# Value projections at 512 columns, last products by column halves, and a queue offset for every stick-breaking head

## The chip, the cores and the metric

One core of one Trainium2 chip runs the kernel. The metric is the device time of one execution in microseconds (us); below, TensorE is PE, VectorE is DVE, ScalarE is ACT, GpSimd is POOL, and SP is the engine that issues most transfers.

## The reference, cut to what matters

Two layers (DEPTH 2) work on 512 tokens of width 1024. Each layer is a half-step SwiGLU, a gated mix of three attentions, and another half-step SwiGLU, each between two RMS norms. All is float32.

```python
for l in range(DEPTH):
    f = _swiglu(_rmsnorm(h, ffn1_pre_g[l]), ffn1_w_gate[l], ffn1_w_up[l], ffn1_w_down[l])
    h = h + 0.5 * _rmsnorm(f, ffn1_post_g[l])
    u = _rmsnorm(h, mix_pre_g[l])
    proj = u @ w_in[l]
    q_sb, k_sb, v_sb, q_fx, k_fx, v_fx, f_logit, q_mem = jnp.split(proj, split_at, axis=-1)
    o_sb = stick_breaking(q_sb, k_sb, v_sb)          # 8 heads of 64
    o_fx = forgetting(q_fx, k_fx, v_fx, log_f)       # 8 heads of 64
    k_mem, v_mem = jnp.split(mem_n @ w_mem_kv[l], 2, axis=-1)
    o_mem = memory(q_mem, k_mem, v_mem)              # 4 heads of 128, 256 memory rows
    merged = g_sb * (o_sb @ w_br_sb[l]) + g_fx * (o_fx @ w_br_fox[l]) + g_mem * (o_mem @ w_br_mem[l])
    h = h + _rmsnorm(merged @ w_out[l], mix_post_g[l])
    f = _swiglu(_rmsnorm(h, ffn2_pre_g[l]), ffn2_w_gate[l], ffn2_w_up[l], ffn2_w_down[l])
    h = h + 0.5 * _rmsnorm(f, ffn2_post_g[l])
```

The values v_sb are 512 columns of `w_in` wide (all eight heads), v_fx as well, and v_mem is the second 512 columns of `w_mem_kv`.

## The kernel before

Every large matrix product is made with three matmuls: each operand is split into a high part (a rounded copy, made by ACT) and a low part (the residue, made by DVE), and `mm3` adds high x high, high x low and low x high in PSUM. `split` makes the two parts. A weight slice of 512 KB is a `Unit`: SP loads it into one of two raw buffers (`raw`), ACT casts it to `wh`, DVE makes the residue `wl` (four buffers each). A square of 128 x 128 numbers is the stationary operand of a matmul; the moving one is up to 512 columns wide.

The order of PE's work is written out by a queue, `Queue` (`Q`). A job in it is a set of units and a generator that emits matmuls; `Q.step` emits the next piece, loads the units of the job that begins, and loads up to four units ahead. Attention heads are chains: a generator yields ("pe", us) for PE work that it just emitted and ("wait", us) for the queued PE work that is to be put in before its next part. `Q.weave` puts chain and queue together, up to a limit in the queue; `Q.past` runs the queue past a job and some microseconds on; `Q.until` runs it to a mark. The engines then run in order, so these offsets set how much other PE work lies between the parts of a head.

The mixing stage of a layer `l`, in order:

- `mem_kv` adds the memory keys (two jobs `keys`, tiles `pmk`, 256 columns of memory rows moving) and the memory values (two jobs `values`, tiles `pmv`, each 256 value columns wide, by `vproj`). The second values job is added from `mixing` by `rest`.
- `mixing` adds the memory queries (`pqm`), then for every head pair p a q and a k projection (`project`, tiles `pq`, `pk`), value projections (`project_v`), and gated merges (`merge`, gate tiles `pg`, product tiles `pb`). Values of two head pairs are made at a time, 256 columns, by `v_half` and `vproj` (tiles `pv`); two token tiles share a bank of PSUM. The forgetting branch's first value job also makes the forget logits and is 264 columns wide (`v_gates`).
- `run` in `mixing` weaves the heads: four memory heads (`mem_head`), eight stick-breaking heads (`stick_head`, pair p and head j, tiles `zs`, `ts`, `pts`, `pvs`), eight forgetting heads (`fox_head`). In a stick-breaking head PE makes the scores `zs` (L966); ACT and DVE turn them into weights in `ts` (L971 to L983); PE transposes them into `pts` (L952, in `transposed`); ACT and DVE split these; PE multiplies with the values into `pvs` (L939, in `attend`).

Between `zs` and `pts` the weave puts in W_SB0 of queued work, plus an entry of W_MORE for three of the heads, and between `pts` and `pvs` W_SB1:

```python
    W_SB0, W_SB1 = 12.0, 4.7
    W_MORE = {(0, 0): -5.5, (NP - 1, 0): 2.0, (NP - 1, 1): 1.0}
```

`down` makes a SwiGLU's last products (tiles `pdc` in the second SwiGLU) and the output projection. Its last two token tiles are made one after the other by `late`, then `Sub.result` squares and scales a tile's half (L549, L554), `rstd` makes the norm's factor, and `Sub.residual` adds into `hm` (L572) and stores (L573).

At the start, `begin` loads tiles of x on SP (L1366, L1369), `Sub.gains` loads the first gain row in two pieces (`grow`, L536) and PE spreads it over the partitions (`gqx`, L540); `warm(n)` issues n matmuls whose result is not used (L1359); `turn` transposes a normed tile (`utx`, L1389).

Of the kernel before, what the change touches and what calls it, by code (L numbers as in the profile page):

```python
# [17 lines left out]
P = 128  # L18
# [4 lines left out]
def kernel(  # L23
# [469 lines left out]
    def rstd(st, a, b=None):  # L493

        s, m, y, w = st[:, a:a + 1], st[:, 3:4], st[:, 4:5], st[:, 5:6]
        if b is None:
            nc.scalar.activation(y, s, AF.Ln, bias=eps_t[:])
            nc.vector.tensor_scalar(m, s, D * EPS, None, ALU.add)
        else:
            nc.vector.tensor_scalar(m, s, st[:, b:b + 1], D * EPS, ALU.add, ALU.add)  # L500
            nc.scalar.activation(y, m, AF.Ln)
        nc.scalar.activation(y, y, AF.Exp, scale=-0.5)

        nc.vector.scalar_tensor_tensor(w, m, y, y, ALU.mult, ALU.mult)
        nc.vector.scalar_tensor_tensor(y, w, -3.0, y, ALU.add, ALU.mult)
        return y

    class Sub:
# [20 lines left out]
        def gains(self, quick=False):  # L529

            if quick:
# [3 lines left out]
                for row, c in zip(rows, HF):  # L535
                    nc.sync.dma_start(row, gain_srcs[i][l:l + 1, c])  # L536
# [23 lines left out]
        def result(self, t, hf, src):  # L560
# [3 lines left out]
            self.scaled(self.fs[t][:, HF[hf]], src, hf)  # L564

# [217 lines left out]
    def down(w, ktiles, act, emit, name, dst, marks, before=None):  # L783
# [23 lines left out]

        def late(uns, hf, t):
            Q.hold = True
# [68 lines left out]
    def mem_kv(l, mn, ks, vs):  # L878
# [3 lines left out]
        def keys(c, un):  # L882
            kt = stile([P, 2, 2, M], "v", f"mk{l}_{c}")
            for m in range(2):
                pt = pbank("mm", f"pmk{l}_{c}_{m}")
                yield from gemm(pt[:, :M], un, m, mact)
                split(kt[:, 0, m], kt[:, 1, m], pt[:, :M])
# [15 lines left out]
    def vproj(units, act, tiles, name):  # L903

        pt = pbank("mm", name)
        for i, t in enumerate(tiles):
            o = pt[:, i * 256:(i + 1) * 256]
            ts_ = slice(t * P, (t + 1) * P)
            for un in units:
                for k in range(un.nk):  # L910
                    ah, al = act(un.k0 + k)
                    first = i == 0 and un.k0 + k == 0
                    nc.tensor.matmul(o, ah[:, ts_], un.h[:, k], start=first, stop=False)
                    nc.tensor.matmul(o, ah[:, ts_], un.l[:, k], start=False, stop=False)
                    nc.tensor.matmul(o, al[:, ts_], un.h[:, k], start=False, stop=(i == 1 and un.k0 + k == ND - 1))
                    yield 768 * PE_US
        return pt
# [14 lines left out]
    def attend(pv, j, vts, pj, tri, ot, name):  # L932

        r, rl, _ = HEAD_ROWS[j]
        for kt in range(NT):
            lo = QLO[kt]
            v = vts[kt // 2][:, 2 * (kt % 2) + pj, 2 * j:2 * j + 2, :].rearrange("p e c -> p (e c)")
# [18 lines left out]
    def stick_head(q, k, vts, pj, j, ot, name, late):  # L956
# [32 lines left out]
        attend(pbank("mm", "pv" + name), j, vts, pj, wt, ot, name)  # L989
# [13 lines left out]
    def fox_head(q, k, vts, pj, j, qk, ot, name, ahead):  # L1003
# [27 lines left out]
        attend(pbank("mm", "pv" + name), j, vts, pj, tri, ot, name)  # L1031
        yield ("pe", 1.2)

    def mem_head(q, ks, vs, hd, ot, name, begun):
# [37 lines left out]
        for kt in range(MT):  # L1072
            c = slice(kt * S, (kt + 1) * S)
            vc = slice((hd % 2) * P, (hd % 2 + 1) * P)
            v = vs[hd // 2]
            mm3(pv[:], v[:, 0, kt, vc], v[:, 1, kt, vc], tri[:, 0, c], tri[:, 1, c], kt == 0, kt == MT - 1)
# [5 lines left out]
    W_MORE = {(0, 0): -5.5, (NP - 1, 0): 2.0, (NP - 1, 1): 1.0}  # L1082
# [30 lines left out]
    def mixing(l, src, ks, vs, rest, dst):  # L1113
# [36 lines left out]
        def v_half(br, c, un):  # L1150
            for i in range(NT // 2):
# [3 lines left out]
                pt = yield from vproj(un, act, (2 * i, 2 * i + 1), f"pv{l}_{br}_{c}_{i}")  # L1155
# [22 lines left out]
        def project_v(br, p):  # L1178

            base = br * 1536 + 1024 + p // 2 * 2 * P  # L1180
            if (br, p) == (1, FOX[0]):
# [62 lines left out]
        marks["values"] = rest()  # L1244
# [8 lines left out]
        marks[heads[0]] = len(Q.jobs)  # L1253
        for i, (br, _) in enumerate(heads):
# [6 lines left out]
            if i % 2 == 0 and i + 2 < len(heads):  # L1261
# [17 lines left out]
        def run():  # L1279
# [5 lines left out]
            def mems():  # L1285
# [13 lines left out]
                for i in range(NMH):  # L1299
# [12 lines left out]
            def stick(p, j):  # L1312
                return stick_head(st["q", 0, p], st["k", 0, p], st["v", 0, p // 2], p % 2, j, st["o", 0][p], f"s{l}_{p}_{j}",
                                  W_MORE.get((p, j), 0.0))

# [8 lines left out]
            def fox(at, j):  # L1324
                pre(at, j)
                p = FOX[at]
                return fox_head(st["q", 1, p], st["k", 1, p], st["v", 1, p // 2], p % 2, j, fx[p, j], st["o", 1][p],
# [33 lines left out]
    def begin():  # L1361
# [38 lines left out]
        with in_order(nc.scalar, nc.vector):  # L1400
# [3 lines left out]
            r = stats(1)  # L1404
            for hf in range(2):
                turn(0, hf)
            warm(3)
# [37 lines left out]
    for l in LAYERS:  # L1445
# [3 lines left out]
        rest = mem_kv(l, mn, *kvs[l])  # L1449
        mb = mixing(l, subs[i + 1], *kvs[l], rest, subs[i + 2])  # L1450
# [38 lines left out]
```

## Time and profile before

| | us |
|---|---|
| median of three runs | 2437.25 |
| lowest and highest | 2437.09, 2437.45 |
| the profiled execution, own time | 2437.36 |
| its span, first to last instruction | 2435.6 |
| PE busy in it | 2422.2 |
| DVE busy | 1545.3 |
| ACT busy | 1172.6 |
| POOL busy | 72.9 |

The rows of the profile come from the one profiled execution; its span starts at 0. A row of instructions gives the start and length in us, engine, line of the kernel, operation, output and inputs by the program's names, shape and count; "idle before" and "<-" name how long the engine had waited and for whom. A matmul's length reaches into the next one, since they are pipelined; the distance between two starts is what one occupies.

### The profile page before, as it was taken

How to read it: one execution, taken by the hardware profiler on the slowest of the kernel's cores; microseconds unless marked ns; L12 is line 12 of the kernel's file. 1: busy time of each engine (PE TensorE's matmuls, PEld its weight loads, DVE VectorE, ACT ScalarE, POOL GpSimd, SP SyncE). 2: the span in 40 equal slices, each digit the busy share in tenths (PEclk: the TensorE clock that was granted, in tenths of full speed). 3: DMA queues.
4: the chain of work that ended last, by engine and by line, in shares of the span. 5: the costliest groups of instructions: out<-in, count | busy, mean ns of one | idle time of the engine just before them, and what ended most of it. 6: DMA issues, size and time to landing. Idle time of an engine off the chain costs nothing.

```text
span 2435.6 us, 30761 instructions
## 1 busy us (share of the span) xinstructions
PE 2422.2 (99%) x12103; PEld 2056.8 (84%) x12103; DVE 1545.3 (63%) x2183; ACT 1172.6 (48%) x1897; POOL 72.9 (3%) x130
## 2 busy tenths in 40 slices
PE   9999999999999999999999999999999999999998
PEld 7888889888888888888888888899888888888887
DVE  5364777677776653646644546776778766445466
ACT  4333365567665443333433333555776655333333
POOL 0000000000110000000000000000001100000000
PEclk9999999999999999999999999999999999999999
DMA  4334445222323433444524344542232234343433
GB/s 140 116 126 130 136 160 154 65 84 70 87 65 119 137 104 112 125 125 127 159 87 136 109 144 131 161 133 70 70 94 73 77 130 130 96 130 108 143 114 129
DMA packets 238597, 280.50 MB, mean 115 GB/s; under 512 B 8666, under 2 KB 188914, under 8 KB 238452
## 3 DMA queue, kind: packets, MB, share of 16 engines
q1 hardware_dynamic: 238356, 278.50, 37.1%
q8 instruction: 95, 1.56, 0.3%
q14 instruction: 50, 0.41, 0.0%
q0 software_dynamic: 96, 0.03, 0.0%
HBM read 272.20 MB, written 6.29 MB: 114 GB/s over the span
## 4 chain that ended last, share of the span: by engine, by line
PE 96%; DVE 2%; ACT 1%; DMA 1%; issue 1%; SPq 0%; DVEq 0%; ACTq 0%
PE pg L214 3%; PE pg L215 3%; PE pg L216 3%; PE pga L214 3%; PE pga L215 3%; PE pgc L214 3%; PE pda L216 3%; PE pda L215 3%; PE pga L216 3%; PE pua L216 3%; PE pua L215 3%; PE puc L214 3%; PE pgc L215 3%; PE puc L216 3%; PE pgc L216 3%; PE puc L215 3%
## 5 line engine op out<-in xcount | busy, mean ns | idle before, releaser
L214 PE MATMUL pg<-us_a,wh_wg 128*128 128x512 f32 x384 | 150.3, 391 | 0.0
L215 PE MATMUL pg<-us_a,wh_wg 128*128 128x512 f32 x384 | 149.8, 390 | 0.0
L216 PE MATMUL pg<-us_a,wl_wg 128*128 128x512 f32 x384 | 149.6, 389 | 0.0
L214 PE MATMUL pgc<-us_b,wh_gc 128*128 128x512 f32 x320 | 124.5, 389 | 0.0
L215 PE MATMUL pgc<-us_b,wh_gc 128*128 128x512 f32 x320 | 124.5, 389 | 0.0
L216 PE MATMUL pgc<-us_b,wl_gc 128*128 128x512 f32 x320 | 124.5, 389 | 0.0
L214 PE MATMUL puc<-us_b,wh_uc 128*128 128x512 f32 x320 | 124.5, 389 | 0.0
L215 PE MATMUL puc<-us_b,wh_uc 128*128 128x512 f32 x320 | 124.5, 389 | 0.0
L216 PE MATMUL puc<-us_b,wl_uc 128*128 128x512 f32 x320 | 124.5, 389 | 0.0
L189 DVE TENSOR_TENSOR wl_uc<-raw_uc,wh_uc 128x1024 fp32r<-128x1024 f32 x44 | 53.9, 1225 | 107.4 <-ACT wh_uc L188 107.4
L189 DVE TENSOR_TENSOR wl_ua<-raw_ua,wh_ua 128x1024 fp32r<-128x1024 f32 x44 | 53.8, 1224 | 99.7 <-ACT wh_ua L188 99.7
L188 ACT CAST wh_uc<-raw_uc 128x1024 fp32r<-128x1024 f32 x44 | 46.3, 1052 | 89.6 <-PE pgc L215 37.5
L189 DVE TENSOR_TENSOR wl_gc<-raw_gc,wh_gc 128x1024 fp32r<-128x1024 f32 x40 | 48.8, 1223 | 62.1 <-ACT wh_gc L188 61.8
L216 PE MATMUL pda<-wh_da,ala 128*128 128x512 f32 x224 | 87.1, 389 | 0.0
L214 PE MATMUL pda<-wh_da,aha 128*128 128x512 f32 x224 | 87.1, 389 | 0.0
L215 PE MATMUL pda<-wl_da,aha 128*128 128x512 f32 x224 | 87.1, 389 | 0.0
L214 PE MATMUL pdc<-wh_dc,ahc 128*128 128x512 f32 x224 | 87.1, 389 | 0.0
L215 PE MATMUL pdc<-wl_dc,ahc 128*128 128x512 f32 x224 | 87.1, 389 | 0.0
L216 PE MATMUL pdc<-wh_dc,alc 128*128 128x512 f32 x224 | 87.1, 389 | 0.0
L188 ACT CAST wh_ua<-raw_ua 128x1024 fp32r<-128x1024 f32 x44 | 46.2, 1051 | 83.7 <-PE pga L215 33.6
L189 DVE TENSOR_TENSOR wl_ga<-raw_ga,wh_ga 128x1024 fp32r<-128x1024 f32 x40 | 48.8, 1223 | 58.4 <-ACT wh_ga L188 58.3
L216 PEld LDWEIGHTS pg<-us_a,wl_wg 128*128 128x128 f32 x384 | 72.1, 188 | 15.1
(466 smaller groups left out, 7235.9 us busy)
## 6 DMA issues: line engine op xcount, KB each, us to landing
raw_da<-in_ffn_w_down_dram SPq DMA_DIRECT2D x58, 512.0 KB, 3.4
raw_dc<-in_ffn_w_down_dram SPq DMA_DIRECT2D x58, 512.0 KB, 3.4
raw_wg<-in_w_gate_dram SPq DMA_DIRECT2D x48, 512.0 KB, 3.5
raw_ga<-in_ffn_w_gate_dram SPq DMA_DIRECT2D x44, 512.0 KB, 3.8
raw_ua<-in_ffn_w_up_dram SPq DMA_DIRECT2D x44, 512.0 KB, 3.9
raw_gc<-in_ffn_w_gate_dram SPq DMA_DIRECT2D x44, 512.0 KB, 3.9
raw_uc<-in_ffn_w_up_dram SPq DMA_DIRECT2D x44, 512.0 KB, 3.8
raw_wo<-in_w_out_dram SPq DMA_DIRECT2D x24, 512.0 KB, 3.4
```

The lines of the kernel that those rows point to most:

```text
L188: both = [nc.scalar.copy(h_ap, src)]
L189: make = lambda: nc.vector.tensor_tensor(l_ap, src, h_ap.bitcast(F32), ALU.subtract)
L214: nc.tensor.matmul(pt, lh, rh, start=start, stop=False, skip_group_check=free)
L215: nc.tensor.matmul(pt, lh, rl, start=False, stop=False, skip_group_check=free)
L216: nc.tensor.matmul(pt, ll, rh, start=False, stop=stop, skip_group_check=free)
```

## The change

Values. `v_all` replaces `v_half` for the stick-breaking branch: one job makes all 512 value columns, a token tile a bank, from four units of two 128-row slices and 512 columns. The two memory values jobs also become 512 columns wide: the jobs now share out the 1024 rows of the product's inner dimension (four slices of 128 each, in two units) in place of the columns, and both are added in `mem_kv`. `v_half` stays for the forgetting branch's second value job, written out with `mm3`. The memory keys' two products of a job share one bank and one split. `attend` takes a function that gives a value tile.

Queue. The first head pair's weave begins only once the value job is through (`marks["v"]`). W_MORE holds two offsets for a head, one for each wait, and names seven of the eight heads.

End. For the very last token tile of the last SwiGLU, `at_last` makes the products in two column halves and `last_part` adds, squares and scales each half; the second half's root takes the other sums as the bias of the Ln, and `hm` is made and stored in three pieces (512, 256 and 256 columns).

Start. The gain row's two loads are issued by ACT; `warm(2)` stands ahead of tile 0's transposes in place of `warm(3)` behind them.

```diff
-    def rstd(st, a, b=None):
+    def rstd(st, a, b=None, pre=None):
...
-        if b is None:
+        if pre is not None:
+            nc.scalar.activation(y, s, AF.Ln, bias=st[:, pre:pre + 1])
+            nc.vector.tensor_scalar(m, s, st[:, pre:pre + 1], None, ALU.add)
+        elif b is None:
...
-                    nc.sync.dma_start(row, gain_srcs[i][l:l + 1, c])
+                    nc.scalar.dma_start(row, gain_srcs[i][l:l + 1, c])
...
+        def last_part(self, t, hf, c, pt, i):
+            f, h, st = self.fs[t], hT[t], self.sf[t]
+            s, fc, w = tmp(f"fe{i}"), f[:, HF[hf]][:, c], slice(0, c.stop - c.start)
+            nc.vector.tensor_tensor(s[:, w], fc, pt, ALU.add)
+            self.squared(s[:, w], st, 2 * i, s[:, S // 2:])
+            nc.vector.scalar_tensor_tensor(fc, s[:, w], RS * (0.5 if self.half else 1.0), self.gp[:, HF[hf]][:, c],
+                                           ALU.mult, ALU.mult)
+            if i == 0:
+                nc.vector.tensor_scalar(st[:, 1:2], st[:, 0:1], st[:, 1:2], D * EPS, ALU.add, ALU.add)
+                return
+            r = rstd(st, 2, pre=1)
+            for hc in (HF[1 - hf], *(slice(HF[hf].start + p.start, HF[hf].start + p.stop) for p in HALVES)):
+                nc.vector.scalar_tensor_tensor(h[:, hc], f[:, hc], r, h[:, hc], ALU.mult, ALU.add)
+                nc.sync.dma_start(out[0, t * P:(t + 1) * P, hc], h[:, hc])
...
+        def at_last(uns, hf, t):
+            parts = [(c, pbank("mm", f"p{name}_{hf}_{t}_{i}")) for i, c in enumerate(HALVES)]
+            for i, (c, pt) in enumerate(parts):
+                for un in uns:
+                    for k in range(un.nk):
+                        kk = un.k0 + k
+                        ah, al = act(kk, slice(t * P, (t + 1) * P))
+                        mm3(pt[:, c], ah, al, un.h[:, k, c], un.l[:, k, c], kk == 0, kk == ktiles - 1)
+                        yield 3 * S // 2 * PE_US
+                dst.last_part(t, hf, c, pt[:, c], i)
...
+            if t == NT - 1 and dst.g_pre is None and hf == 0:
+                yield from at_last(uns, hf, t)
+                return
...
-        def values(c, un):
-            vt = stile([P, 2, MT, 256], "v", f"mv{l}_{c}")
-            pt = yield from vproj(un, mact, range(MT), f"pmv{l}_{c}")
-            split(vt[:, 0].rearrange("p t c -> p (t c)"), vt[:, 1].rearrange("p t c -> p (t c)"), pt[:])
-            vs.append(vt)
+        def values(un):
+            if un[0].k0 == 0:
+                pvs.extend(pbank("mm", f"pmv{l}_{t}") for t in range(MT))
+            for un1 in un:
+                for t, pt in enumerate(pvs):
+                    yield from vproj(un1, mact, t, pt)
+            if un[0].k0 > 0:
+                for t, pt in enumerate(pvs):
+                    vs.append(stile([P, 2, S], "v", f"mv{l}_{t}"))
+                    split(vs[t][:, 0], vs[t][:, 1], pt[:])
...
-        un = [wpair(w_mem_kv[l], ND, 512 + c * 256, f"mv{l}_{c}") for c in range(2)]
-        Q.add(un[0], lambda: values(0, un[0]))
-        return lambda: Q.add(un[1], lambda: values(1, un[1]))
+        un = [Unit(w_mem_kv[l], k, 2, S, S, f"mv{l}_{k}") for k in range(0, ND, 2)]
+        Q.add(un[:2], lambda: values(un[:2]))
+        return Q.add(un[2:], lambda: values(un[2:]))
+    def vproj(un, act, t, pt):
+        ts_ = slice(t * P, (t + 1) * P)
+        for k in range(un.nk):
+            kk = un.k0 + k
+            ah, al = act(kk)
+            mm3(pt[:, :un.ncol], ah[:, ts_], al[:, ts_], un.h[:, k], un.l[:, k], kk == 0, kk == ND - 1)
+            yield 3 * un.ncol * PE_US
...
-        yield ("wait", W_SB0 + late)
+        yield ("wait", W_SB0 + late[0])
...
-        yield ("wait", W_SB1)
+        yield ("wait", W_SB1 + late[1])
...
-    W_MORE = {(0, 0): -5.5, (NP - 1, 0): 2.0, (NP - 1, 1): 1.0}
+    W_MORE = {(0, 0): (-8.0, 0.0), (0, 1): (-1.5, -1.0), (1, 1): (0.5, -0.5), (2, 0): (-1.0, 0.0),
+              (2, 1): (-0.5, 1.5), (NP - 1, 0): (0.0, 2.5), (NP - 1, 1): (1.0, 0.0)}
...
+        def v_all(br, un):
+            for t in range(NT):
+                vt = stile([P, 4, 4, HD], "v", f"v{l}_{br}_{t}")
+                st.setdefault(("v", br), []).append(vt)
+                pt = pbank("mm", f"pv{l}_{br}_{t}")
+                for un1 in un:
+                    yield from vproj(un1, act, t, pt)
+                split(vt[:, :, 0:4:3, :], vt[:, :, 1:3, :], pt[:].rearrange("p (a e c) -> p a e c", a=4, e=2))
...
+            if br == 0:
+                un = [Unit(w_in[l], k, 2, base, S, f"v{l}_{br}_{k}") for k in range(0, ND, 2)]
+                Q.add(un, lambda: v_all(br, un))
...
-            if i % 2 == 0 and i + 2 < len(heads):
+            if i in (2, 4):
                 project_v(*heads[i + 2])
...
-                            Q.past(marks[0, 0], W_K, marks[0, 1])
+                            Q.past(marks[0, 0], W_K + 2.5, marks[0, 1])
...
                 Q.past(marks[0, p], W_K, limits[p][0])
+                if p == 0:
+                    Q.until(marks["v"])
...
             r = stats(1)
+            warm(2)
             for hf in range(2):
                 turn(0, hf)
-            warm(3)
```

More of the change, by code (lines that the diff above doesn't have):

```diff
@@ L883, in keys @@
             kt = stile([P, 2, 2, M], "v", f"mk{l}_{c}")
+            pt = pbank("mm", f"pmk{l}_{c}")
             for m in range(2):
[L885 to L894 removed]
+                for un1 in un:
+                    for k in range(un1.nk):
+                        kk, cols = un1.k0 + k, slice(m * P, (m + 1) * P)
+                        ah, al = mact(kk)
+                        mm3(pt[:, m * M:(m + 1) * M], un1.h[:, k, cols], un1.l[:, k, cols], ah, al, m == 0 and kk == 0,
+                            m == 1 and kk == ND - 1, free=True)
+                        yield 3 * M * PE_US
+            split(kt[:, 0], kt[:, 1], pt[:].rearrange("p (e m) -> p e m", e=2))
+            ks.append(kt)
+        pvs = []
+        def values(un):
[8 more added lines that the diff above has]
+                    split(vs[t][:, 0], vs[t][:, 1], pt[:])
         for c in range(2):
@@ L954, in transposed, with stick_head @@
         return tri
-    def stick_head(q, k, vts, pj, j, ot, name, late):
+    def stick_head(q, k, value, j, ot, name, late):
         banks = [[(i, 0)] for i in reversed(range(2, NT))] + [[(1, 0), (0, 2 * P)]]
@@ L1001, in fox_pre, with fox_head @@
         return qk
-    def fox_head(q, k, vts, pj, j, qk, ot, name, ahead):
+    def fox_head(q, k, value, j, qk, ot, name, ahead):
         rc = slice(0, 104 if j == 0 else P)
@@ L1242, in merge @@
             return Q.add(ub, run)
-        marks["values"] = rest()
+        marks["values"] = values
         for c in range(2):
```

55 lines of the change are left out of this document (25 added, 30 removed).

## The prediction

> **What bounds the kernel.** I read the page first (busy time, chain), then PE's waits, then the stages that the diff touches in time.
>
> ```profile
> PE 2422.2 (99%) x12103; PEld 2056.8 (84%) x12103; DVE 1545.3 (63%) x2183; ACT 1172.6 (48%) x1897; POOL 72.9 (3%) x130
> PE 96%; DVE 2%; ACT 1%; DMA 1%; issue 1%; SPq 0%; DVEq 0%; ACTq 0%
> PE pvs L939 <- DVE pts L189: 1.1, 2, 0.6
> PE pwo L215 <- DVE wl_wo L189: 0.9, 1, 0.9
> ```
>
> PE is busy for 99% of the span and makes 96% of the chain; its waits are single microseconds (pvs waited 1.1 us in two places, one in each layer; pwo's 0.9 lies in a stage that the diff leaves). So time comes only from four places: what a matmul occupies of PE, the few waits, and the chains before PE's first and after its last steady work.
>
> A group's mean duration of one matmul (283 ns at 256 columns) overlaps its neighbour, so the cost is the distance between starts:
>
> ```profile
> 439.58 0.28 PE L914 MATMUL pv<-wl_v,us_a 128*128 128x256 f32 x1
> 444.98 0.28 PE L914 MATMUL pv<-wl_v,us_a 128*128 128x256 f32 x1
> ...
> 457.74 0.39 PE L214 MATMUL pk<-us_a,wh_k 128*128 128x512 f32 x1
> 461.82 0.39 PE L214 MATMUL pvm<-ptm,mv 128*128 128x512 f32 x1
> ```
>
> Between the first two lie 45 steps: 5.40/45 = 0.1200 us for 256 columns. Between the last two lie 18: 4.08/18 = 0.2267 us for 512. Two narrow ones cost 0.2400, so one wide one in their place saves 13.3 ns.
>
> **1. Values with 512 columns.** The forms before:
>
> ```profile
> L913 PE MATMUL pv<-wh_v,us_a 128*128 128x256 f32 x192 | 54.6, 284 | 0.0
> L913 PE MATMUL pmv<-wh_mv,mn 128*128 128x256 f32 x64 | 18.4, 288 | 0.0
> ```
>
> L914 and L915 issue as many, so there are 576 narrow products for pv and 192 for pmv. Two thirds of the pv ones are stick-breaking's (two of three narrow projections a layer): 384. They become 192 wide ones, pmv's 192 become 96. That is 288 pairs x 13.3 ns = **-3.84 us**, all on PE and so on the chain (rounding of the starts: -3.7 to -4.0). The Trainium skill ("TensorE: Matmul & The Clock Gate", Back-to-back issue gap) speaks against this: its warm gap N/2.4 + 2.5 ns leaves 2.5 ns a pair, as an estimate 0.7 us in all. The two measured distances differ by 106.7 ns for 256 columns, which leaves 13.3 ns fixed in either, so here the trace decides.
>
> Memory keys keep their 192 narrow products; two of them now share a bank and one 512-column split replaces two 256-column ones, on ACT and DVE beside PE: nothing. The weights stay 512 KB a load, as many loads, on SP in the same order but for the values' place, so DMA adds nothing. What could show is the four weight buffers, all held by one value job. The order of after has the fourth slice's first product 18 wide matmuls (4.08 us) behind the k product that frees its buffer, and the next q weights' buffer free 18 matmuls before the value job ends. A load's two halves cost:
>
> ```profile
> L188 ACT CAST wh_uc<-raw_uc 128x1024 fp32r<-128x1024 f32 x44 | 46.3, 1052 | 89.6 <-PE pgc L215 37.5
> L189 DVE TENSOR_TENSOR wl_uc<-raw_uc,wh_uc 128x1024 fp32r<-128x1024 f32 x44 | 53.9, 1225 | 107.4 <-ACT wh_uc L188 107.4
> ```
>
> 1.05 + 1.23 = 2.3 us, so 1.8 us of queueing on ACT or DVE is covered: nothing, and rival 3 if that cover is gone.
>
> **2. Queued work set for every head.** Each stick-breaking head runs scores (zs), a long chain on ACT and DVE, transposes (pts), their split, and products (pvs); queued projections fill PE in between. What PE lost before:
>
> ```profile
> 537.32 0.39 PE L216 MATMUL pk<-us_a,wl_k 128*128 128x512 f32 x1
> ...
> 537.81 1.31 PE pts L952 x10
> ...
> 609.88 0.39 PE L939 MATMUL pvs<-pts,v 128*128 128x512 f32 x1
> 610.89 1.42 PE L939 MATMUL pvs<-pts,v 128*128 128x512 f32 x7 [0.62 <-DVE pts L189]
> ```
>
> Head (1,1) lost 0.49 - 0.23 = 0.26 us ahead of its transposes; head (3,0) lost 1.01 - 0.23 = 0.78 at its products. In layer 1 the pvs wait is 1.1 - 0.62 = 0.5 (0.16 less, so 0.66 lost, its slow start counted as in layer 0), and I take 0.26 again for (1,1). Together 1.96 us. These can go. Whether they do is cover against need. Cover is the PE work that the order puts between a head's zs and pts, in wide matmuls. Before: 57 for (1,1) = 12.9 us, and 12 (2.7 us) between (3,0)'s pts and pvs. After: 60 for (1,1) = 13.6 us, and 36 (8.2 us) for (3,0). But (0,1) falls from 13.4 us to 51 = 11.56, (2,0) from 12.9 to 11.56, (3,0)'s first part from 15.0 to 12.9, and (0,1)'s second from 5.6 to 4.1. Needs, from the end of zs to the last Exp on ACT:
>
> ```profile
> 478.68 1.30 PE zs L966 x8
> ...
> 478.51 1.46 PE L966 MATMUL zs<-k,q 128*128 128x512 f32 x8
> 492.15 0.52 ACT L983 ACTIVATE ts<-ts 128x384 f32<-128x384 f32 x1 [1.02 <-DVE ts L982]
> ...
> 523.30 1.46 PE L966 MATMUL zs<-k,q 128*128 128x512 f32 x8
> 537.25 0.51 ACT L983 ACTIVATE ts<-ts 128x384 f32<-128x384 f32 x1
> ...
> 589.76 1.46 PE L966 MATMUL zs<-k,q 128*128 128x512 f32 x8
> 604.24 0.53 ACT L983 ACTIVATE ts<-ts 128x384 f32<-128x384 f32 x1
> ```
>
> A zs set occupies PE for 1.30 us. (0,1): 492.67 - 479.81 = 12.9 us. (1,1): 537.76 - 524.60 = 13.2. (3,0): 604.77 - 591.06 = 13.7. By the order, (0,1)'s chain after is no longer interleaved with two weight residues on DVE (2 x 1.23 gone) but keeps nearly its ACT work; its need falls by 1 to 2.5, say to 11.4 against 11.56. (1,1) keeps its DVE work and gains one 512-column step of ACT: 13.2 to 13.8 against 13.6. (3,0) had the forget gate's sums ahead of it on ACT and now has them between its steps: about 13 against 12.9. So three heads end within some tenths of their cover. I take 0.25 us a layer left (0 to 1.2): 1.96 - 0.5 = **-1.5 us** (-2.0 to +0.4).
>
> **3. Start.** The gain row's two small loads go from SP to ACT's queue; two warming matmuls stand ahead of tile 0's transposes in place of three behind them.
>
> ```profile
> 0.80 1.28 ACT L85 ACT_TABLE_LOAD   x1 [0.80 <-PEq L1478]
> 1.24 0.60 SPq L536 DMA_DIRECT2D grow<-in_ffn_pre_g_dram  x2
> 1.88 0.36 SPq L1369 DMA_DIRECT2D hx<-in_x_dram  x1
> 4.42 1.06 ACT L549 ACTIVATE fx<-hx 128x1024 f32<-128x1024 f32 x1 [2.34 <-DMA hx<-in_x_dram]
> ...
> 1.88 6.22 DMA hx<-in_x_dram
> ...
> 4.37 1.95 PE L540 MATMUL gqx<-grow,ones 1*128 1x512 f32 x4 [0.31 <-DMA grow<-in_ffn_pre_g_dram]
> 7.57 1.72 PE L1389 MATMUL utx<-ident,fx 128*128 128x128 f32 x7 [1.26 <-DVE fx L1398]
> 8.12 1.06 ACT L549 ACTIVATE fx<-hx 128x1024 f32<-128x1024 f32 x1 [1.99 <-DMA hx<-in_x_dram]
> ```
>
> The chain goes through the second x tile: issued at 1.88, landed at 8.1, then ACT. Its issue moves up by 0.64 us, to 1.24; what of it arrives depends on the transfers that share the wires, 0 to 0.64, and I take two thirds: **-0.4 us**. The gain row, now behind the 1.28 us table load, is issued near 2.1 to 2.7 instead of 1.24 to 1.84; ACT's own first work waits for an x tile until 4.42, so the two issues delay nothing there. Its spread on PE moves from 4.4..6.3 to about 5.2..7.2, still ahead of tile 0's transposes (7.57), but the two warm matmuls add about 1 us: these transposes begin near 8.1. ACT cannot take them before it is through tile 1's square (9.2 before, about 8.8 after) and its root, so that is hidden; were it not, it costs up to 0.5.
>
> **4. The very last tile.** 18 wide products become 36 narrow ones: 36 x 0.120 - 18 x 0.2267 = +0.24 us of PE; in return half of the tile's add, square and scale can run under the second half.
>
> ```profile
> 2424.17 0.69 DVE L680 TENSOR_TENSOR fc<-fc,pdc 128x512 f32<-128x512 f32 x1 [1.79 <-PE pdc L216]
> 2426.82 1.41 DVE L572 SCALAR_TENSOR_TENSOR hm<-fc,nfc,hm 128x512 f32<-128x512 f32 x2
> 2428.25 0.69 DVE L680 TENSOR_TENSOR fc<-fc,pdc 128x512 f32<-128x512 f32 x1
> 2430.90 1.41 DVE L572 SCALAR_TENSOR_TENSOR hm<-fc,nfc,hm 128x512 f32<-128x512 f32 x2
> 2431.68 0.99 SPq L573 DMA_DIRECT2D out_dram<-hm  x2
> ...
> L189 DVE TENSOR_TENSOR v<-pv,v x20: 400/670/693, 446.0 to 1872.5; 128x512 fp32r<-128x512 f32 x12, 128x256 fp32r<-128x256 f32 x8
> ```
>
> But DVE is full there. Counted from tile 2's add (2424.17 = 0), it was busy with tile 2 until 4.06 and took tile 3's sum at 4.08. After, it also does tile 3's first half (add and scale, about 0.41 each by the 0.40 row, and a 0.2 step) ahead of or between tile 2's steps: 4.06 + 1.0 = 5.1, while the second half's products end at 4.3. So the second add starts at 5.1, not 4.3. From tile 3's add to its hm it took 2430.90 - 2428.25 = 2.65 us; at half the width the add is 0.28 shorter, the square I estimate as much, and one small step of 0.2 goes: 1.9. hm then takes 0.7 + 0.4 + 0.4 in place of 1.41. The last hm ends near 8.5 against 2430.90 + 1.41 - 2424.17 = 8.14 before. The last store is half as large and issued 0.4 later. I take **+0.2 us** (-0.3 to +0.6).
>
> **Sum** against the profiled execution, 2437.36 us (span 2435.6 and 1.8 around it): -3.84 - 1.5 - 0.4 + 0.2 = -5.5, so 2431.8; the median shown (2437.25) lies 0.1 lower, so **2431.7 us**. The forecast's own range, from the bounds: 2430.4 to 2432.9. About 0.2% (4.9 us, here 2432.4) is what a measurement of this kernel can tell from no change.
>
> **Rivals.**
>
> *1. The waits only change heads.* The covers of (0,1), (2,0) and (3,0) are shorter than before; if ACT and DVE run each chain as slowly as then, (0,1) alone misses 12.9 - 11.56 = 1.3 us a layer and the 1.96 are spent again. For: three heads within tenths. Against: (0,1)'s lost DVE work. -3.84 - 0.4 + 0.2 = -4.0: 2433.3. Chance 0.12.
>
> *2. The start turns cold.*
>
> ```profile
> 6.00:8.00 2.00, 0.74 (x3) 0.46 (x3) 1.70 (x4) 0.13 (x1) 1.20 (x3) 0.89 0.86 259
> 8.00:10.00 2.00, 2.00 (x10) 1.54 (x9) 0.38 (x3) 1.82 (x5) 0.00 (x0) 0.50 1.07 388
> 10.00:12.00 2.00, 1.56 (x8) 0.59 (x7) 1.93 (x5) 1.86 (x4) 0.00 (x0) 0.76 1.05 371
> ```
>
> PE's granted clock (the column behind POOL) was 0.50 from 8 to 10; the 0.89 and 0.76 beside it put the low stretch from about 7.6 to 11.0. The three warming matmuls stood in it, behind the transposes of 7.57. After, only transposes stand there. If the half clock then lies over the first 3.4 us of steady products, it costs 1.7 us and the start's 0.4 goes under it: -3.8, 2433.5. The Trainium skill (same page, What's actually happening) has the clock halve after an idle window of about 3.4 us, free-running; the low stretch agrees in length. Against: the two matmuls close the gap between 6.3 and 7.6 that preceded it. Chance 0.11.
>
> *3. The value job starves what follows it.* All four weight buffers belong to it. If ACT or DVE stands over 1.8 us behind at its end, the next q weights come late; if the buffers were in effect free only at its end, PE would wait 2.3 us at its fourth slice and again at the next job, 2.3 x 2 x 2 layers = 9.2: +3.7, **slower**, 2441.0. Against: the order shows the buffers free slice by slice. Chance 0.05.
>
> *4. The change does not do what it says for PE:* the 13.3 ns belong to the place, not to the instruction, and a wide value product takes two narrow ones' time. Without the 3.84: -1.7, 2435.6. The gap formula of the Trainium skill (named under 1) would end near it: as an estimate -0.7 in place of -3.84, 2434.9. Against: k and pvm products, 512 wide, in the same stage, at 0.2267. Chance 0.04.
>
> **Numbers.** The forecast keeps 0.68, of which 0.58 lies over 0.2% faster and 0.10 within. Rivals 1, 2 and 4 are within (0.27). Faster 0.58, same 0.37, slower 0.05. The range reaches up to rivals 1 and 2 and, below, past the forecast's own end for a tail that gains as well: 2430.0 to 2434.0.
>
> **What would show it.** Right: 288 wide forms of pv and pmv at 0.227 us between starts; PE's instructions fewer by some 270; no pvs wait of 0.6; the second hx landing near 7.7; fe's second add on DVE 0.8 us behind PE's last product. Wrong: waits of PE at pts of (0,1), (1,1) or (3,0); granted clock at 0.5 beyond 11.5 us; PE waiting for wh_v, wl_v or wl_q.

## The result: 3.74 us faster, 0.15%, and the profile after

The changed kernel takes 2433.34 us (median of 22 runs, 2432.57 to 2434.65) where the kernel before took 2437.08 beside it (22 runs, 2436.05 to 2438.26): 3.74 us less, a ratio of 0.9985 with a 95% interval of 0.9978 to 0.9991. The forecast was 2431.7 with a range of 2430.0 to 2434.0. The time lies in the range, 1.6 us above the forecast, and the gain is under the 0.2% to which the forecast had given its largest chance. The interval leaves out "no change", so 0.2% was too coarse a limit for what 22 runs of each can tell. 2433.3 was the time of rival 1, and its mechanism, waits that only change heads, is what happened; that the time is met to a tenth is luck, since terms that the rival did not have cancel (below).

The profiled execution took 2433.56 us, with a span of 2431.8. From its page, and from the view of PE's waits (total us, times, longest us):

```profile
PE 2420.0 (100%) x11832; PEld 2044.3 (84%) x11832; DVE 1549.7 (64%) x2183; ACT 1173.6 (48%) x1895; POOL 78.0 (3%) x130
```

```profile
PE pts L996 <- ACT ts L1027: 2.2, 4, 0.6
...
PE mt L906 <- DVE fa L755: 0.5, 1, 0.5
```

PE issues 271 instructions fewer (12103 before). The waits at pvs and pwo are gone; four waits at pts have come, and one at the memory rows' transposes (mt).

**Values.** The new forms in the view of groups, and the first and last of 33 in the timeline:

```profile
L215 PE MATMUL pv<-wl_v,us_a 128*128 128x512 f32 x64 | 24.9, 389 | 0.0
...
L215 PE MATMUL pmv<-wl_mv,mn 128*128 128x512 f32 x32 | 12.5, 390 | 0.0
```

```profile
439.69 0.39 PE L214 MATMUL pv<-wh_v,us_a 128*128 128x512 f32 x1
...
446.94 0.39 PE L216 MATMUL pv<-wh_v,us_a 128*128 128x512 f32 x1
```

Each of the three lines of `mm3` issues as many, so there are 192 + 96 wide products, and 7.25/32 = 0.2266 us between starts. That is the forecast's price: -3.84 us. The memory values, which are a stretch of their own, took 12.69 us a layer from their first product to the next projection's in place of 13.24: 0.55 less, where that price gives 0.64.

**Heads.** What precedes the transposes of head (0,1) in layer 0:

```profile
476.71 1.46 PE L1010 MATMUL zs<-k,q 128*128 128x512 f32 x8
...
478.91 1.05 ACT L188 CAST wh_q<-raw_q 128x1024 fp32r<-128x1024 f32 x1
...
479.99 1.23 DVE L189 TENSOR_TENSOR wl_q<-raw_q,wh_q 128x1024 fp32r<-128x1024 f32 x1 [1.78 <-ACT wh_q L188]
...
480.37 0.73 ACT L1017 ACTIVATE ts<-ts,one_t 128x512 f32<-128x512 f32 x1
...
481.13 0.68 DVE L189 TENSOR_TENSOR o<-ss,o 64x512 fp32r<-64x512 f32 x1
481.73 1.25 DVE L1018 SCALAR_TENSOR_TENSOR ts<-zs,ts 128x512 f32<-128x512 f32 x2
...
489.37 0.39 PE L216 MATMUL pg<-us_a,wl_wg 128*128 128x512 f32 x1
489.76 0.51 ACT L1027 ACTIVATE ts<-ts 128x384 f32<-128x384 f32 x1
490.32 1.31 PE L996 MATMUL pts<-ident,ts 128*128 128x128 f32 x10 [0.56 <-ACT ts L1027]
```

and head (1,0), whose scores start at 496.88:

```profile
500.69 1.06 ACT L191 ACTIVATE wh_wg<-raw_wg 128x1024 fp32r<-128x1024 f32 x1
...
501.66 0.71 ACT L1017 ACTIVATE ts<-ts,one_t 128x512 f32<-128x512 f32 x1
...
501.79 1.23 DVE L192 SCALAR_TENSOR_TENSOR wl_wg<-raw_wg,wh_wg 128x1024 fp32r<-128x1024 f32 x1 [0.40 <-ACT wh_wg L191]
502.93 0.68 DVE L1018 SCALAR_TENSOR_TENSOR ts<-zs,ts 128x512 f32<-128x512 f32 x1
...
507.89 1.20 DVE L189 TENSOR_TENSOR wl_wb<-raw_wb,wh_wb 128x1024 fp32r<-128x1024 f32 x1
...
511.26 0.52 ACT L1027 ACTIVATE ts<-ts 128x384 f32<-128x384 f32 x1
511.84 1.31 PE L996 MATMUL pts<-ident,ts 128*128 128x128 f32 x10 [0.56 <-ACT ts L1027]
```

(0,1) needs 490.27 - 478.01 = 12.3 us from the end of its scores to its last Exp and has 11.56 of cover; (1,0) needs 511.78 - 498.18 = 13.6 and has 12.92. Each loses 490.32 - 489.37 - 0.23 = 0.72 us, in both layers: 2.88 us where the kernel before lost 1.96. In both cases a weight unit stands ahead of the chain's first DVE step (L1018): ACT casts it ahead of the chain's third ACT step (L1017), and DVE is at its residue of 1.2 us when that step ends. L1018 then starts 0.6 us after L1017's end in either head. For (1,0) this is new. In the kernel before:

```profile
501.22 1.46 PE L966 MATMUL zs<-k,q 128*128 128x512 f32 x8
...
504.19 0.72 ACT L973 ACTIVATE ts<-ts,one_t 128x512 f32<-128x512 f32 x1
...
504.94 0.69 DVE L974 SCALAR_TENSOR_TENSOR ts<-zs,ts 128x512 f32<-128x512 f32 x1
...
513.72 0.53 ACT L983 ACTIVATE ts<-ts 128x384 f32<-128x384 f32 x1
```

Its need was 514.25 - 502.52 = 11.7 us. The first DVE step came 2.4 us after the scores' end, now it comes 4.75 after it, and 1.8 of the difference is there already at the third ACT step (3.5 in place of 1.7).

**Start.**

```profile
1.25 0.42 SPq L1438 DMA_DIRECT2D hx<-in_x_dram  x1
...
3.99 3.78 PE L546 MATMUL gqx<-grow,ones 1*128 1x512 f32 x4
...
6.17 1.04 ACT L555 ACTIVATE fx<-hx 128x1024 f32<-128x1024 f32 x1
...
7.70 1.03 PE L1428 MATMUL warm<-warm 128*128 128x512 bf16 x2
8.52 3.62 PE L1458 MATMUL utx<-ident,fx 128*128 128x128 f32 x16
...
13.98 1.22 PE L680 MATMUL pga<-us_x,w_ga 128*128 128x256 f32 x8 [0.21 <-ACT w_ga L188]
```

ACT squares the second x tile at 6.17 in place of 8.12, but the gain spread (gqx) takes 3.78 us in place of 1.95, and the chain now goes through PE: spread, warming, transposes. The second batch of PE's first products starts at 13.98; before it was 14.11.

**End.**

```profile
2420.38 0.69 DVE L703 TENSOR_TENSOR fc<-fc,pdc 128x512 f32<-128x512 f32 x1 [1.80 <-PE pdc L216]
...
2422.72 0.42 DVE L576 TENSOR_TENSOR fe<-fc,pdc 128x256 f32<-128x256 f32 x1
...
2424.38 0.28 PE L216 MATMUL pdc<-wh_dc,hidc 128*128 128x256 f32 x1
2424.96 0.41 DVE L576 TENSOR_TENSOR fe<-fc,pdc 128x256 f32<-128x256 f32 x1
...
2426.96 1.54 DVE L586 SCALAR_TENSOR_TENSOR hm<-fc,nfc,hm 128x512 f32<-128x512 f32 x3
```

The first of two hm steps of tile 2 starts at 2423.51. From tile 2's add to the span's end: 2431.8 - 2420.38 = 11.42 us; before 2435.6 - 2424.17 = 11.43.

**The two profiled executions, place by place** (in us, from PE's first start in a place to its first start behind it, so with the slower matmuls that follow a wait): columns -3.84 by their price; heads +0.60 (3.10 lost in place of 2.50; the gaps alone, as the forecast counted them, give 2.88 - 1.96 = +0.92); the pwo wait gone, -1.18; the memory rows' transposes +1.08 (0.88 in layer 0, 0.20 in layer 1); two stumbles of 0.17 in forgetting heads gone, -0.34; start -0.13; end -0.01. Together -3.82, and 2437.36 - 2433.56 = 3.80.

### The profile page after: what moved, and what is told of

It is laid out like the page before. It is cut to its first block, busy times and chain, and to the rows that moved or that the text cites. A ratio compares the mean times of both kernels' runs of the same rounds, so it can differ in the third digit from the quotient of the medians.

```text
span 2431.8 us, 30227 instructions
## 1 busy us (share of the span) xinstructions
PE 2420.0 (100%) x11832; PEld 2044.3 (84%) x11832; DVE 1549.7 (64%) x2183; ACT 1173.6 (48%) x1895; POOL 78.0 (3%) x130
## 4 chain that ended last, share of the span: by engine, by line
PE 95%; DVE 2%; ACT 1%; DMA 0%; issue 0%; DVEq 0%; ACTq 0%
PE pg L214 3%; PE pg L215 3%; PE pg L216 3%; PE pgc L215 3%; PE puc L215 3%; PE pgc L214 3%; PE pgc L216 3%; PE puc L214 3%; PE puc L216 3%; PE pga L214 3%; PE pga L215 3%; PE pga L216 3%; PE pdc L214 3%; PE pdc L215 3%; PE pdc L216 3%; PE pda L216 3%
```

## The experiments

The theory: the wide columns give what was forecast, and the heads' waits are cover against need, each head with a need of its own that depends on which weight residues and gate steps the queue puts on DVE and ACT beside it. The rivals: the stock of queued work is fixed, so waits only change heads; ACT bounds the chains; the start or the end carries the rest. Times are medians; the kernel before took 2437.3 to 2437.6 beside these runs.

### The wide values alone

```diff
-    W_MORE = {(0, 0): (-8.0, 0.0), (0, 1): (-1.5, -1.0), (1, 1): (0.5, -0.5), (2, 0): (-1.0, 0.0),
-              (2, 1): (-0.5, 1.5), (NP - 1, 0): (0.0, 2.5), (NP - 1, 1): (1.0, 0.0)}
+    W_MORE = {(0, 0): (-5.5, 0.0), (NP - 1, 0): (2.0, 0.0), (NP - 1, 1): (1.0, 0.0)}
...
-                            Q.past(marks[0, 0], W_K + 2.5, marks[0, 1])
+                            Q.past(marks[0, 0], W_K, marks[0, 1])
```

Start and last products were also those of before.

> The 512-column value projections alone: head cover, start and very last products as in the kernel before. Theory (the columns give -3.84 on PE, and the cover table is a part that the wide projections need because they shift the queued work): by the order, head (3,0) is left with 3 wide matmuls (0.7 us) between its transposes and its products, where 12 (2.7 us) left a wait of 0.6 before; its need is then about 3.5 us, so it loses about 2.8 us a layer there instead of 0.7: -3.84 + 4.2 = +0.3 against the kernel before, 2437.5 (2436 to 2439), with a pvs wait of PE of some 5 us in all. Rival (the columns give nothing and the change's gain is the start and the queue): 2441. Second rival (the queue settings are worth little): 2433.5, no pvs wait over 1.5.

2437.95 us, a ratio of 1.0002 (0.9993 to 1.0011). PE's waits at the products:

```profile
PE pvs L983 <- ACT pts L188: 3.1, 4, 1.0
...
PE pvs L983 <- DVE pts L189: 1.1, 2, 0.6
```

As the theory said: without the offsets the columns' gain goes into (3,0)'s products, 4.2 us of idle time where there were 1.1. So the offsets and the columns are one change: with the old offsets the queue leaves 0.7 us of work at that place.

### More cover for (0,1) and (1,0)

```diff
-    W_MORE = {(0, 0): (-8.0, 0.0), (0, 1): (-1.5, -1.0), (1, 1): (0.5, -0.5), (2, 0): (-1.0, 0.0),
+    W_MORE = {(0, 0): (-8.0, 0.0), (0, 1): (0.0, -1.0), (1, 0): (1.5, 0.0), (1, 1): (0.5, -0.5), (2, 0): (-1.0, 0.0),
```

> The changed kernel with 1.5 us more queued work asked for by heads (0,1) and (1,0): by the order 57 wide matmuls (12.92 us) cover (0,1) in place of 51 (11.56), and 60 (13.60) and more, 14.3 us in all, cover (1,0) in place of 57 (12.92). Theory (each head has its own need, (0,1) 12.3 and (1,0) 13.6 us, and the changed kernel asked too little for these two): PE's pts wait of 2.2 us goes, 4 x 0.72 = 2.9 us less than the changed kernel, 2430.5 (2430.0 to 2431.3). Rival (a fixed amount of queued work: what two heads get another lacks): the same time as the changed kernel within 0.5 us, 2433.3, with waits at pts or pvs of heads (2,0), (2,1) or (3,0) instead.

2433.24 us, 0.9982 (0.9973 to 0.9990): no better. The rival won this run: the four waits are gone and (3,0) waits instead, in both layers.

```profile
PE pts L996 <- ACT ts L1027: 2.5, 2, 1.5
```

(3,0)'s cover is the same 12.92 us as in the changed kernel, which lost nothing there. What moved is its need. First here, then in the changed kernel:

```profile
586.07 0.74 DVE L1148 SCALAR_TENSOR_TENSOR fa<-pfl,nbfor,fa 8x512 f32<-8x512 f32 x1 [0.54 <-ACT fa L1147]
586.36 1.46 PE L1010 MATMUL zs<-k,q 128*128 128x512 f32 x8
...
588.81 0.62 ACT L1152 CAST cs<-fb 8x512 fp32r<-8x512 f32 x1 [0.93 <-DVE fb L1149]
...
590.18 0.63 ACT L1016 ACTIVATE ts<-ts 128x512 f32<-128x512 f32 x1
...
601.73 1.31 PE L996 MATMUL pts<-ident,ts 128*128 128x128 f32 x10 [0.97 <-ACT ts L1027]
```

```profile
585.88 1.45 PE L1010 MATMUL zs<-k,q 128*128 128x512 f32 x8
...
588.95 0.63 ACT L1016 ACTIVATE ts<-ts 128x512 f32<-128x512 f32 x1
```

Work drawn earlier brings the forget gate's sums ahead of (3,0)'s chain: ACT stands 0.93 us for one of them, with the chain's second step (L1016) behind it, 3.8 us after the scores' start in place of 3.1.

### Without two residues

```diff
+            elif self.name in ("q0_0_2", "q1_0_2", "wg0_2_1_4", "wg1_2_1_4"):
+                self.h = self.l = stile(shape, self.tags[0], "wh_" + self.name)[:]
+                return nc.scalar.activation(self.h, raw, AF.Copy, scale=1.0 if self.scale is None else self.scale)
```

> The changed kernel, leaving out in each layer the low part of two weight units: the 1.2 us residue on DVE that stands ahead of head (0,1)'s first chain step (third unit of the q weights) and the one ahead of head (1,0)'s (fifth unit of a gate weight); the high part is used in its place, so the matmuls and the covers stay. Theory (these residues delay the chains by about 1.2 us each): all four waits of PE ahead of the transposes of (0,1) and (1,0) vanish; pts wait under 0.3 in place of 2.2 us, time 2.5 to 2.9 us under the changed kernel. Rival (the chains are bound by ACT, and DVE has slack): the waits stay at 0.5 to 0.6 each, and the time stays within 0.5 us.

2430.96 us (one run), 2.6 under the changed kernel's profiled run, whose start it shares (gqx 3.78 in both), and no wait at pts in the list of PE's waits. In head (0,1):

```profile
481.33 0.69 DVE L1021 SCALAR_TENSOR_TENSOR ts<-zs,ts 128x512 f32<-128x512 f32 x1
...
488.23 0.53 ACT L1030 ACTIVATE ts<-ts 128x384 f32<-128x384 f32 x1
```

The last Exp ends at 488.76 in place of 490.27, though the scores end no earlier. The needs fall from 12.3 to 10.5 and from 13.6 to 12.4 us, while the covers are those of the changed kernel (11.6 and 12.9), and only DVE work was taken away. So without these two residues a layer the four waits don't come, and the rival falls. How a residue costs that much is shown in part: the first DVE step moves by only 0.6 and 0.3 us (to 3.1 and 4.4 after the scores' end), and the rest comes behind it, where DVE also takes the steps in another order (here one L1021, then the first part's scan; in the changed kernel two L1018, then two scans). What the order alone is worth was not run. (1,0)'s need stays above the 11.7 of the kernel before; the weight's cast on ACT is still there.

### Cover for (3,0) too

```diff
-              (2, 1): (-0.5, 1.5), (NP - 1, 0): (0.0, 2.5), (NP - 1, 1): (1.0, 0.0)}
+              (2, 1): (-0.5, 1.5), (NP - 1, 0): (1.5, 1.0), (NP - 1, 1): (1.0, 0.0)}
```

> As the kernel with more queued work for (0,1) and (1,0), and 1.5 us more for (3,0), so that its cover is 14.28 us too; what stands between its transposes and its products falls from 6.1 to 4.8 us. In that kernel (3,0) waited 1.0 and 1.5 us at 12.92, because the forget gate's steps now stand ahead of its first chain step: needs of 14.0 and 14.5. Theory (every head can be given its cover; nothing is taken from another that lacks it): the pts wait falls from 2.5 to 0.2 us or less, 2.6 us less than the changed kernel, 2430.6 (2430 to 2431.5). Rival (a fixed stock: the next head, (3,1) or its products, pays): 2433.2, with 2 us of waits at pvs of (3,0) or pts of (3,1).

2432.19 us, 0.9978 (0.9969 to 0.9987). The profiled execution, 2431.22 us with a span of 2429.5, has no wait at pts or pvs, 2.3 us of span less than the changed kernel at the same start (gqx 3.78). So in this execution the stock is not fixed, and the rival falls. The median lies 1.0 higher than that execution and above the theory's range. With (2.2, 0.5) for (3,0), which gives it 14.96 us:

> As the kernel with 14.28 us for (3,0), but 14.96 us, and 4.1 us between its transposes and its products. That kernel showed no pts wait in its profiled execution, 2431.2 us, but a median of 2432.2. Theory (in other executions (3,0) still waits some tenths, since its needs were 14.0 and 14.5): the median comes down to 2431.2 (2430.5 to 2431.7), no pts or pvs wait. Rival (the spread comes from the start and not from this head): 2432.2 again.

2430.82 us, 0.9973 (0.9963 to 0.9983), where the theory had 2431.2; the rival (2432.2) is out by 1.4. But the theory's sign, no wait at pts, did not come. Its profiled execution is its slowest (2432.47) and still shows one wait:

```profile
PE pts L996 <- ACT ts L1027: 0.4, 1, 0.4
```

It is (3,0) in layer 1, at 14.96 us of cover, and in the same kernel without the warming matmuls too (0.3). With 14.96 the head needs 15.5 us, where it needed 14.3 in the kernel with 14.28 and 12.6 in the changed kernel. So the need of this head grows with what is put beside it and is not quite met. Why the median fell by 1.4 us is not shown: of the two profiled executions, alike at the start (gqx 3.78), the one with 14.96 is the slower by 1.25. This kernel, 6.7 us under the kernel before, is faster than both kernels of this change, and each of its 9 runs is under each of the changed kernel's 22.

### The end

```diff
-            if t == NT - 1 and dst.g_pre is None and hf == 0:
+            if False:
```

> The changed kernel with the very last products of 512 columns in one piece. Theory (the column halves cost 0.24 on PE and give back as much behind it: from tile 2's add to the span's end 11.42 us against 11.43 in the kernel before): the same time as the changed kernel, 2433.3, and 11.4 us from that add to the end. Rival (the forecast's +0.2 was right and something else hides it): 0.2 us less, 11.2 from that add to the end.

2433.31 us, 0.9984 (0.9975 to 0.9993): the same time. From tile 2's add (2420.61) to the span's end (2432.1) 11.49 us. The column halves are worth nothing here, as the theory said.

### The start

The start of before in the changed kernel, then the new start in the kernel before (gain row on ACT's queue, `warm(2)` ahead):

```diff
-                    nc.scalar.dma_start(row, gain_srcs[i][l:l + 1, c])
+                    nc.sync.dma_start(row, gain_srcs[i][l:l + 1, c])
...
-            warm(2)
             for hf in range(2):
                 turn(0, hf)
+            warm(3)
```

> The changed kernel with the start of the kernel before: gain row on SP's queue, three warming matmuls behind tile 0's transposes. Theory (the new start gave 0.13 us, by the second batch of PE's first products at 13.98 in place of 14.11 us): +0.1 us, 2433.4 (2433.0 to 2434.0), and that batch at 14.1. Rival (the half clock of the start lies under what follows, so the start is worth the forecast 0.4 or more): +0.4 to +1.5 us.

> The kernel before with the new start alone (gain row on ACT's queue, two warming matmuls ahead of tile 0's transposes). Theory (the start is worth 0.85 us, by executions of one kind: with the gain spread taking 3.8 us the second batch of PE's first products came at 13.98 in place of 14.82, with 2.0 us at 13.2 in place of 14.11; the forecast's 0.4 was half of it): 0.85 us under the kernel before, 2436.4 (2435.9 to 2437.0). Rival (the forecast's size, or the 0.13 that the two first profiles show): 0.1 to 0.4 us. It also shows a second execution of the old steady work: whether the 1.05 us that the kernel before lost at a pwo product belongs to it (theory: yes, the wait is there again) or to chance.

The first: 2434.17 us, 0.9986 (0.9977 to 0.9995), 3.28 under the kernel before where the changed kernel was 3.74 under it: the new start is worth 0.5, so the theory's 0.1 was missed. The second: 2437.33, 0.9998 (0.9990 to 1.0007): 0.2, so the theory's 0.85 was missed. With the larger covers the old start was put in once more:

> The kernel with more queued work for (0,1), (1,0) and (3,0) (14.96 us), with the start of the kernel before. What is open: the new start came out at 0.8 to 1.1 us beside the changed kernel and at 0.2 beside the kernel before. Theory (0.85, as executions of one kind showed): 0.85 over 2430.8, 2431.7 (2431.3 to 2432.3). Rival (0.2): 2431.0, within 0.3 of the kernel with the new start.

2432.36 us, 0.9978 (0.9969 to 0.9987), 5.28 under the kernel before where the kernel with the new start was 6.67 under it: 1.4, more than theory and rival had. The three sizes, 0.2, 0.5 and 1.4, have a mean of 0.7; each interval reaches some 2 us to either side, so no closer value is settled, and none of them is clear of zero by itself.

Why executions differ can be seen. First the changed kernel with the old start, then the kernel with more cover for (0,1) and (1,0), with the new one:

```profile
4.76 3.75 PE L546 MATMUL gqx<-grow,ones 1*128 1x512 f32 x4 [0.70 <-DMA grow<-in_ffn_pre_g_dram]
...
14.82 1.21 PE L680 MATMUL pga<-us_x,w_ga 128*128 128x256 f32 x8 [0.32 <-ACT w_ga L188]
```

```profile
3.99 2.01 PE L546 MATMUL gqx<-grow,ones 1*128 1x512 f32 x4
...
13.22 1.21 PE L680 MATMUL pga<-us_x,w_ga 128*128 128x256 f32 x8 [0.21 <-ACT w_ga L188]
```

The gain spread takes 2.0 to 2.2 us in some profiled executions and 3.8 in others, with either start. With 3.8 the second batch came at 13.98 (new start, three kernels) against 14.82 and 14.58 (old); with 2.0 at 13.22 against 14.11 and 13.51. So in like executions the new start gains 0.3 to 0.9. The kernel before was profiled with 1.95 and the changed one with 3.78, so the pair shows only 0.13.

The clock tells the two kinds apart. In the six executions with 2.0 to 2.2 the trace's records begin with the full clock at 4.1 to 4.6 us, have 0.50 from 7.5 or 8.0 on, and the full clock again from 10.9 to 11.4 (14.8 in one). In the eight with 3.8 the first record is the full clock at 12.2 to 13.5 (12.55 in the changed kernel), and the view of stretches shows 1.00 ahead of it where no record is. PE was at half rate until then: the changed kernel's 16 transposes (utx) started 3.20/15 = 0.213 us apart up to 11.72, and the next 8, from 18.88 to 19.65, 0.110. So the half rate lasts beyond 11.5, a sign of being wrong that the prediction named, and the first products (12.56) just miss it. It comes with the old start too, in two of four profiled executions, so it is not the change's alone; whether the new start with its warming matmuls brings it more often (six of seven) is open.

Which part gains was asked with the loads alone back on SP (the first line of the diff):

> The changed kernel with the gain row's two loads back on SP's queue, the warming matmuls left in their new place. Theory (the start's gain comes from the second x tile, which is issued and lands earlier): the second x tile lands near 8 us again and the second batch of PE's first products comes 0.8 later, at 14.1 or 14.8; +0.8 us against the changed kernel. Rival (it comes from the place of the warming matmuls): the batch stays at 13.2 or 14.0.

2434.42 us, 0.9987 (0.9978 to 0.9996), 3.07 under the kernel before where the changed kernel was 3.74 under it: 0.7. ACT's square of the second x tile comes at 7.39. The first products start at 12.26, 0.47 later than in the execution with a spread of 2.0 above (11.79), and what follows them 1.16 later. So the later x tile, by the queue's place, accounts for 0.5 of these 1.16 us; the other 0.7 has another cause:

```profile
8.00:10.00 2.00, 1.06 (x5) 0.66 (x4) 0.94 (x4) 1.94 (x7) 0.00 (x0) 0.50 1.06 388
10.00:12.00 2.00, 1.52 (x7) 1.55 (x8) 1.59 (x3) 1.41 (x3) 0.00 (x0) 0.50 1.07 370
12.00:14.00 2.00, 2.00 (x10) 1.77 (x9) 1.76 (x3) 1.74 (x4) 0.00 (x0) 0.50 1.05 359
14.00:16.00 2.00, 2.00 (x15) 1.99 (x15) 2.00 (x4) 1.94 (x5) 0.00 (x0) 0.80 0.52 158
```

The granted clock (behind POOL) is 0.50 from 8 to 14, into the first products, twice the low stretch of the kernel before. This is rival 2's mechanism, in a kernel that has the two warming matmuls ahead and a late x tile. Whether the late tile brought the second low stretch, and how the median's 0.7 is shared, is not shown.

Last, without the two warming matmuls, in the changed kernel and in the one with 14.96 us for (3,0):

```diff
-            warm(2)
```

> The changed kernel without the two warming matmuls ahead of tile 0's transposes. Theory (they stand on the chain where PE is at its half rate early, 0.96 us there, and beside the second x tile's square where it is not, 0.6 us): executions whose gain spread takes 3.8 us gain 0.8, the second batch of PE's first products at 13.2 in place of 13.98; those whose spread takes 2.0 us stay at 13.2; the median falls by 0.4 (0 to 0.8). Rival (the matmuls keep the half rate away from what follows): the transposes and first products run at half rate later than 12 us, and the batch comes at 14.5 or later, +0.5 or more.

> The same without the two warming matmuls. Theory (they are worth nothing at the median; where the gain spread takes 3.8 us they stand on the chain with 0.96): 0 to 0.4 under that kernel, 2431.0 (2430.3 to 2431.5); if its profiled execution has the spread at 3.8 us, the second batch of PE's first products comes at 13.2 in place of 13.98. Rival (they keep the half rate off): slower by 0.5, the batch at 14.5 or later.

2433.12 us, 0.9982 (0.9974 to 0.9991), and 2430.72, 0.9974 (0.9963 to 0.9984): both 0.1 to 0.2 under their kernels, which the intervals don't resolve. Both profiled executions had a spread of 2.1 us and the batch at 13.18 and 13.14, the value with the warming (13.22), not the rival's 14.5. What the warming costs where the spread takes 3.8 us was not seen and stays open.

## Why the prediction was right in range and 1.6 us too low

- **1. Columns: right.** Forecast -3.84, measured distance 0.2266 for 512, so rival 4 falls. No wait for wh_v, wl_v or wl_q came, so rival 3 falls. The memory values' part came out at 1.10 in place of 1.28. By the warm gap that the Trainium skill ("TensorE: Matmul & The Clock Gate", Back-to-back issue gap) states for a matmul by itself, an estimate of 0.7 us would have been left of it; the two measured distances differ from it here.
- **2. Queue: the step that failed.** Forecast -1.5, measured +0.6 (+0.92 by the forecast's own count), beyond its bound of +0.4. The sentence "its need falls by 1 to 2.5, say to 11.4 against 11.56" put (0,1) at 11.4; it was 12.3. The working counted the residues that no longer lay between the chain's steps and left out the cast and the residue that now stand ahead of the first DVE step. Head (1,0), the one head without an offset, was not costed at all, since its cover did not change; its need did, from 11.7 to 13.6 against 12.9. (1,1), (2,0) and (3,0), the other heads named as tight, lost nothing: 13.4 of 13.6, 10.8 of 11.6, 11.9 and 12.6 of 12.9. Rival 1 had the mechanism and, for (0,1) alone, the price of 1.3 us a layer; it was 0.72 at each of two heads, 1.44. The experiments with residues left out and with more cover show that cover against need is the cause, and the size; the share of the casts is argued from the rows.
- **3. Start: right in sign, off in size and in a reason.** Forecast -0.4; in like executions -0.3 to -0.9, by medians -0.2 to -1.4, in the profiled pair -0.13. "The second hx landing near 7.7" was too late: ACT used it at 6.17. The gain row was not behind the table load: ACT's queue issued it at 0.83, and the spread began at 3.99, before the forecast's 5.2. Rival 2's half rate was there in the profiled execution, but ahead of the first products, so its 1.7 us did not come.
- **4. End: mis-sized.** Forecast +0.2, measured 0.0. "4.06 + 1.0 = 5.1" for the second add was 2424.96 - 2420.38 = 4.58: the first half's add and scale stood between tile 2's small dependent steps, and from the add to hm tile 2 took 2423.51 - 2420.38 = 3.13 us in place of 2.65 before. So they cost 0.48, where the working added their full 0.8. The old end gave the same time.
- **Not in the sum:** -1.18 at pwo, +1.08 at mt, -0.34 in forgetting heads, together -0.44. The pwo wait belongs to the order before: it is there again in the kernel before with the new start (0.6 us), and neither the wide values alone nor the changed kernel has it; two variants with other offsets showed 0.2 and 0.3 in layer 1. Why the wide values remove it was not followed up. mt waited 0.2 to 0.7 in every profiled execution but that of the kernel before, also in the kernel before with the new start (0.2), so it does not come from the wide values alone.
- **Luck, and the sum's range.** Without these -0.44 the time would have been 2433.8, just inside the range. Rival 1's 2433.3 was met because heads that lost more than it had and a start that gave less stand against them. And the forecast's own upper end, 2432.9, does not follow from its bounds: -3.7 + 0.4 + 0 + 0.6 = -2.7 is 2434.6.

Had the queue given its -1.5 and the rest come as it did, the sum would have been -5.9; with cover for three heads a kernel measured -6.7.

## What to carry to other kernels

Cover against need has to be worked out for every chain, also for those whose cover doesn't change: what is queued beside a chain brings casts and residues of its own onto the engines that the chain uses, and one that stands ahead of the chain's first step on an engine counts as well as one between two steps. When one chain is given more cover, look again at all that follow, since work drawn earlier changes their neighbours; here a head with the same 12.92 us of cover went from no wait to 1.5 us. A gain in the columns alone was worth nothing until the order around it was set again.

## What the runs showed of the hardware

- With the text of the start unchanged, and with either start, PE's four spread matmuls took 2.0 to 2.2 us in six profiled executions and 3.8 in eight, and PE first got its full clock at 4.1 to 4.6 us in the six and at 12.2 to 13.5 in the eight. Behind an early one came a stretch of 0.50 of 3.41 us (6.83 in the kernel with the gain row on SP). The Trainium skill ("TensorE: Matmul & The Clock Gate", What's actually happening) has a clock gate with a free-running window of 3.4 us, which does not begin with the kernel; two rates from one text agree with that, and the low stretches are one such window and two.
- Two transfers of 2 KB ahead of the second x tile's load in SP's queue, 0.6 us of issue, moved ACT's first use of that tile by 0.8 to 2.1 us: 7.18 to 8.12 in the five executions that have them, 6.03 to 6.42 in the nine that don't.
